# A hybrid encoder block on one core: x transposed through ScalarE's queue, the second FFN product two chunks behind, and transposes in whole groups

## The chip, the core and the metric

The kernel runs on one core of one Trainium2 chip. The time is device microseconds of that core for one execution of the whole block. A core has five engines with a queue each: TensorE (PE in the profile, with PEld for its weight loads), VectorE (DVE), ScalarE (ACT), GpSimd (POOL) and SyncE (SP, which here only issues transfers). Each works through its own queue in order and waits on semaphores of the others.

## The reference

One layer on 256 tokens of width 1024, in float32:

```python
h = rmsnorm(x, ffn1_pre_g);  x = x + 0.5 * rmsnorm(swiglu(h, ffn1_w_in, ffn1_w_down), ffn1_post_g)
h = rmsnorm(x, mix_pre_g);   # one input projection: HGRN2 recurrence and forgetting attention
y = sigmoid(gate_A) * (A @ w_branch_a) + sigmoid(gate_B) * (B @ w_branch_b)
x = x + rmsnorm(y @ w_out, mix_post_g)
x = x + rmsnorm(mem_cross_attention(rmsnorm(x, mem_pre_g), rmsnorm(mem, mem_kv_g), ...), mem_post_g)
h = rmsnorm(x, ffn2_pre_g);  x = x + 0.5 * rmsnorm(swiglu(h, ffn2_w_in, ffn2_w_down), ffn2_post_g)

def swiglu(h, w_in, w_down):
    gate, up = jnp.split(h @ w_in, 2, axis=-1)      # 1024 -> 2 x 2816
    return (jax.nn.silu(gate) * up) @ w_down        # 2816 -> 1024
```

The change touches the head of the kernel (the first norm and the start of the first FFN), both FFNs, and one small step of the mixing stage (the lower bounds of the recurrence's forget gate, a softmax over two rows of logits).

## The kernel before

**Numbers.** Every large product is made of three matmuls: both operands are split into `hi` (rounded to the matmul's format) and `lo` (the rest), and hi x hi, hi x lo and lo x hi are added up in PSUM.

**Weights.** All weights lie in 260 units of 128 x 1024 floats (512 KB). `unit` (L109) issues one transfer on SyncE (L117) into a `raw` tile, casts it to `hi` on ScalarE (L118) and subtracts for `lo` on VectorE (L119). There are 4 `raw` buffers and 8 each of `hi` and `lo`; so a transfer waits until VectorE is done with the unit four before it.

**The norm.** The first product doesn't wait for the norm's statistics. Its input is x^T times the gain (`gain_split`, L245: `hi` on ScalarE, `lo` on VectorE), and the factor per token (`rstd`) is applied when the product is evacuated. `rstd_x` takes the sum of squares of x on ScalarE (L222) and a Newton iteration of small steps on VectorE (L206 to L218).

**The head** (L181 to L216 and L390 to L412): five float32 matmuls of `ones` on TensorE for warming and one Exp on ScalarE; the columns `cols_s` (all gains, the logits of the lower bounds, gate biases) on ScalarE's queue; `fbias` and the masks on GpSimd's. SyncE issues in turn a quarter of x^T and a weight unit, and behind these x itself (`xs`, 1 MB). The lower bounds of the forget gate (`le`, `lbv`, `olb`) follow, with an Exp on ScalarE.

**An FFN** (`ffn`, L288). The 2816 channels go in 11 chunks of 256. A chunk's first product has 24 matmuls of 512 columns per token half h (L153, `proj_tok`); `act_evac` (L298) makes `sg` (Silu on ScalarE) and `at` (times the other half, on VectorE); `act_T` (L305) transposes `at` in two 128 x 128 pieces on TensorE and splits the result into the stationary operand `act` of the second product. `down` (L336) is a chunk's second product, 12 matmuls per half into four PSUM banks `acc`. In the first FFN, `act_first` (L320) does both halves of chunks 0 and 1 together, as units arrive, and chunk 0's evacuation is called right after it. From chunk 1 on the second product of chunk c-1 follows the first product of chunk c; the last four chunks' second products are kept for the end, one token half after the other, so that the closing norm of one half lies beside the other half's matmuls.

**The order.** The tile framework's planner sets each engine's order ahead of the run: of the instructions whose inputs its own estimate of durations has ready, it issues the one with the highest priority, as a rule the earliest in the program. `after(i)` (L80) gives a block high priority and puts its TensorE instructions behind matmul number i of the program; the constants L_ACT = 15, L_F1, L_IA and so on count such matmuls. `late` and `flush` (L294) hold a chunk's transposes back until a later product is being written, with a due place 16 and 17 matmuls into it. PSUM has 4 `acc` banks, 2 `mm` banks and 2 `tr` banks.

Of the kernel before, what the change touches and what calls it, by code (L numbers as in the profile page):

```python
# [9 lines left out]
F32 = mybir.dt.float32  # L10
# [6 lines left out]
P = 128  # L17
# [26 lines left out]
WARM = 5  # L44
# [18 lines left out]
def block_kernel(ctx: ExitStack, tc: tile.TileContext, wts, x_in, xT_in, mem_in, memT_in, cols, rows, fbias, masks, out):  # L63
# [39 lines left out]
    def trp():  # L103
        return pp.tile([P, 512], F32, tag="tr", name=nm("tr"), bufs=2)


    cache = {}

    def unit(name, i, parts=1):  # L109
        u = _AT[name] + i  # L110
        if u not in cache:
            raw = wp.tile([P, D], F32, tag="raw", name=nm("raw"), bufs=4)
            hi = wp.tile([P, D], F32R, tag="hi", name=nm("hi"), bufs=8)
            lo = wp.tile([P, D], F32R, tag="lo", name=nm("lo"), bufs=8)
            for a in range(0, D, D // parts):
                cut = slice(a, a + D // parts)
                nc.sync.dma_start(raw[:, cut], wts[u][:, cut])  # L117
                S.copy(hi[:, cut], raw[:, cut])  # L118
                V.tensor_tensor(out=lo[:, cut], in0=raw[:, cut], in1=hi[:, cut].bitcast(F32), op=ALU.subtract)  # L119
            cache[u] = (hi, lo)  # L120
        return cache[u]
# [65 lines left out]
    S.activation(warm, ones[:, 0:1], AF.Exp)  # L187
    wps = trp()
    for _ in range(WARM):
        MM(wps[:, :P], ones, ones, start=True, stop=True)  # L190
    cols_s = cp.tile([P, 80], F32, name="cols_s")
    S.dma_start(cols_s, cols)
    xs = cp.tile([P, 2, D], F32, name="xs")
    fb_s = cp.tile([8, 1], F32, name="fb_s")
    G.dma_start(fb_s, fbias)
    masks_s = cp.tile([P, len(LEVELS), 64], I32, name="masks_s")
    G.dma_start(masks_s, masks)
# [47 lines left out]
    def gain_split(X, kb, src, g, a=0, b=T):  # L245
        gs = cols_s[:, g + kb : g + kb + 1]
        S.activation(X.hi(kb, a, b), src, AF.Copy, scale=gs)  # L247
        V.scalar_tensor_tensor(out=X.lo(kb, a, b), in0=src, scalar=gs, in1=X.hi(kb, a, b).bitcast(F32), op0=ALU.mult, op1=ALU.subtract)  # L248
# [39 lines left out]
    def ffn(w_in, w_dn, X, r2, n_tok, i_row, first_half, second_half=None):  # L288


        acts = {}
        late = []

        def flush(n):  # L294
            while late:
                late.pop(0)(n)

        def act_evac(ps, c, h):  # L298
            sg = sp.tile([P, FC], F32, tag="c1", name=nm("sg"), bufs=4)
            S.activation(sg, ps[:, :FC], AF.Silu, scale=r2[h])  # L300
            a = sp.tile([P, FC], F32, tag="c1", name=nm("at"), bufs=4)
            V.scalar_tensor_tensor(out=a, in0=ps[:, FC:], scalar=r2[h], in1=sg, op0=ALU.mult, op1=ALU.mult)  # L302
            late.append(lambda m: act_T(a, h, acts[c], m))

        def act_T(a, h, act, m):  # L305
            tr = trp()
            for j in range(2):
                with after(m + 1 + j):
                    PE.transpose(tr[:, j * P : (j + 1) * P], a[:, j * P : (j + 1) * P], ident)  # L309
            with tc.high_priority():  # L310
                split(act[:, 0, :, h * P : (h + 1) * P], act[:, 1, :, h * P : (h + 1) * P], tr[:, :FC].rearrange("p (j t) -> p j t", j=2))
# [8 lines left out]
        def act_first(c, bank):  # L320

            n = len(log)
            u = chunk(w_in, c)
            outs = [bank(), bank()]
            for kb in range(KB):
                wh, wl = blk(u, kb)
                for h in range(2):
                    a, b = h * P, h * P + P
                    MM(outs[h], X.hi(kb, a, b), wh, start=(kb == 0), stop=False)
                    MM(outs[h], X.hi(kb, a, b), wl, start=False, stop=False)  # L330
                    MM(outs[h], X.lo(kb, a, b), wh, start=False, stop=(kb == KB - 1))
            flush(n + L_ACT)
            for h in range(2):
                act_evac(outs[h], c, h)
# [14 lines left out]
        for h in range(2):  # L349
            m = len(log)  # L350
            for c in range(n_tok):
                act_tok(c, h)
            if h == 0 and n_tok:
                second_half(m)
        accs = None
        done = 0
        for c in range(n_tok, NFF):
            acts[c] = m4([P, 2, 2, T], F32R, "act")
            if c < 2:
                act_first(c, (acc, mm)[c])  # L360
            else:
                for h in range(2):
                    act_tok(c, h)
            if c == 6:
                grow = load_row(i_row)
            if accs is None and c:
                accs = [[acc(), acc()], [acc(), acc()]]
            while done < min(c, NFF - STAG):
                n = len(log)
                for h in range(2):  # L370
                    down(done, h)
                done += 1
                flush(n + L_ACT)
# [14 lines left out]

    X1 = Pair()
    for j in range(4):  # L390
        xT = sp.tile([P, 2, T], F32, tag="z2", name=nm("xT"), bufs=3)
        nc.sync.dma_start(xT, xT_in[:, 2 * j : 2 * j + 2, :])
        unit("f1_in", j, 2 if j == 0 else 1)
        for i in range(2):
            gain_split(X1, 2 * j + i, xT[:, i], G_F1)
    for h in range(2):
        nc.sync.dma_start(xs[:, h], x_in[:, h])
    r1 = [rstd_x(x_halves(h)) for h in range(2)]
# [12 lines left out]
    V.tensor_tensor(out=lbv, in0=le[:, 0:8], in1=lsum, op=ALU.mult)  # L411
    V.tensor_scalar(out=olb, in0=lbv, scalar1=-1.0, scalar2=1.0, op0=ALU.mult, op1=ALU.add)  # L412
# [9 lines left out]

    ffn("f1_in", "f1_dn", X1, r1, 0, 0, lambda m: half(X2, r2, 0, G_MIX, m + L_F1))


    iv = [m4([P, 2, 512], n="iv") for _ in range(2)]
    for h in range(2):
        m = len(log)
        for c in range(2):
            ps = mm()  # L430
            proj_tok(ps, X2, chunk("i_a", c), h)
            S.activation(iv[c][:, h, :], ps, AF.Copy, scale=r2[h])
        if h == 0:
            half(X2, r2, 1, G_MIX, m + L_IA)
    row2 = row_of(r2)

# [465 lines left out]
def _layout(inputs):  # L902
# [41 lines left out]
    def col(v):  # L944
# [14 lines left out]
        "wts": wts, "x": nat(a["x"]), "xT": tra(a["x"]), "mem": nat(a["mem"]), "memT": tra(a["mem"]),  # L959
# [19 lines left out]
```

## Time and profile before

| | |
|---|---|
| median of 3 runs | 815.61 us (815.0 to 817.06) |
| the profiled execution | 817.39 us |
| its span, first to last instruction | 815.6 us |
| TensorE busy | 796.6 us, 98% |
| VectorE, ScalarE busy | 522.5 us (64%), 418.5 us (51%) |
| moved by DMA | 146.91 MB, mean 180 GB/s |

Times in the views count from the first instruction. TensorE's busy time is a union of modelled spans; matmuls overlap, so the distance between their starts tells the pace. Lines name the kernel's source (L77 is every matmul, L117 to L119 every weight unit, L309 the transposes of an FFN's chunk, L256 the transposes of x behind a norm); a tile's name tells which operation is meant.

### The profile page before, as it was taken

The page shows a single profiled execution, that of the slowest core. Times are in us where ns is not written, and L with a number is a line of the kernel's source. Part 1 is how long each engine was busy: PE and PEld are TensorE (multiplying, and loading weights), DVE is VectorE, ACT ScalarE, POOL GpSimd, SP SyncE. Part 2 cuts the span into 40 slices and gives each one's busy share as a digit, 9 for nine tenths or more (in the row PEclk, how much of TensorE's full clock was granted, in tenths as well). Part 3 has the DMA queues.
Part 4 walks back from the last instruction along what each step waited for, and adds up shares of the span by engine and source line. Part 5 has one row for each costly group of instructions (what it writes and reads, how often), then busy time and mean ns, then how long its engine had stood idle before and what let it go on. Part 6 is the DMA issues. An engine that isn't in the chain of part 4 may idle for free.

```text
span 815.6 us, 13560 instructions
## 1 busy us (share of the span) xinstructions
PE 796.6 (98%) x5404; PEld 697.3 (85%) x5404; DVE 522.5 (64%) x858; ACT 418.5 (51%) x659; POOL 9.5 (1%) x22
## 2 busy tenths in 40 slices
PE   7999999999999999999999999999999999999996
PEld 5788888887799889998999998999887788888884
DVE  6764555447776897578585466975748755545544
ACT  7644544436565345347675345744636644544531
POOL 0000000000000000100000000000000000000000
PEclk9999999999999999999999999999999999999999
DMA  8675566454464554652466447355426564565421
GB/s 322 244 249 177 173 207 214 161 201 155 151 203 173 174 182 140 201 179 104 155 209 230 149 163 258 134 179 205 153 79 207 190 217 161 185 215 204 168 79 52
DMA packets 41087, 146.91 MB, mean 180 GB/s; under 512 B 4744, under 2 KB 4752, under 8 KB 41024
## 3 DMA queue, kind: packets, MB, share of 16 engines
q1 hardware_dynamic: 40320, 144.20, 51.5%
q0 software_dynamic: 560, 1.81, 0.8%
q8 instruction: 42, 0.69, 0.3%
q14 instruction: 21, 0.17, 0.1%
q10 hardware_dynamic: 144, 0.04, 0.0%
HBM read 144.97 MB, written 1.06 MB: 179 GB/s over the span
## 4 chain that ended last, share of the span: by engine, by line
PE 87%; DVE 5%; DMA 4%; ACT 2%; issue 2%; SPq 0%; DVEq 0%; ACTq 0%
PE mm L77 64%; PE acc L77 20%; DMA raw<-in_wts_dram 3%; DVE lo L119 2%; PE tr L309 1%; PE tr L77 1%; DMA xs<-in_x_dram 1%; ACT junk L222 1%; DVE xs L283 1%; PE tr L256 1%; DVE t L211 1%; DMA cols_s<-in_cols_dram 0%; DVE y L213 0%; ACT hi L118 0%; DVE post L279 0%
## 5 line engine op out<-in xcount | busy, mean ns | idle before, releaser
L119 DVE TENSOR_TENSOR lo<-raw,hi 128x1024 fp32r<-128x1024 f32 (+1 forms) x262 | 317.0, 1221 | 128.1 <-ACT hi L118 124.3
L118 ACT CAST hi<-raw 128x1024 fp32r<-128x1024 f32 (+1 forms) x262 | 269.1, 1046 | 156.8 <-PE mm L77 80.1
L77 PE MATMUL mm<-hi,hT 128*128 128x512 f32 x464 | 183.7, 397 | 2.2 <-ACT hT L247 1.1
L77 PE MATMUL mm<-hT,hi 128*128 128x256 f32 x648 | 183.7, 284 | 0.1
L77 PE MATMUL mm<-hT,lo 128*128 128x256 f32 x648 | 183.7, 284 | 0.0
L77 PE MATMUL mm<-lT,hi 128*128 128x256 f32 x648 | 183.7, 283 | 0.0
L77 PE MATMUL mm<-hi,lT 128*128 128x512 f32 x464 | 183.5, 396 | 0.0
L77 PE MATMUL mm<-lo,hT 128*128 128x512 f32 x464 | 181.5, 391 | 0.5 <-DVE lo L119 0.5
L77 PEld LDWEIGHTS mm<-lT,hi 128*128 128x128 f32 x648 | 124.3, 192 | 0.3 <-issue 0.2
L77 PEld LDWEIGHTS mm<-hT,hi 128*128 128x128 f32 x648 | 124.3, 192 | 0.1
L77 PEld LDWEIGHTS mm<-hT,lo 128*128 128x128 f32 x648 | 124.3, 192 | 0.1
L77 PE MATMUL acc<-hi,act 128*128 128x512 f32 x352 | 114.4, 397 | 0.0
L77 PEld LDWEIGHTS mm<-hi,hT 128*128 128x128 f32 x464 | 87.0, 188 | 22.3 <-ACT hT L247 2.4
L77 PEld LDWEIGHTS mm<-hi,lT 128*128 128x128 f32 x464 | 87.2, 188 | 19.7 <-DVE lT L248 0.3
L77 PEld LDWEIGHTS mm<-lo,hT 128*128 128x128 f32 x464 | 87.2, 188 | 17.6 <-DVE lo L119 1.0
L77 PEld LDWEIGHTS acc<-hi,act 128*128 128x128 f32 x352 | 66.2, 188 | 14.9
L77 PE MATMUL acc<-lo,act 128*128 128x512 f32 x176 | 68.7, 390 | 0.0
L300 ACT ACTIVATE sg<-mm,rstd 128x256 f32<-128x256 f32 x42 | 19.9, 474 | 62.8 <-PE mm L77 62.8
L302 DVE SCALAR_TENSOR_TENSOR at<-mm,rstd,sg 128x256 f32<-128x256 f32 x42 | 20.1, 480 | 49.7 <-ACT sg L300 49.6
L77 PEld LDWEIGHTS acc<-lo,act 128*128 128x128 f32 x176 | 33.1, 188 | 6.3
L77 PE MATMUL acc<-hi,hT 128*128 128x512 f32 x80 | 32.0, 405 | 2.8 <-ACT hi L118 2.7
L77 PE MATMUL acc<-lo,hT 128*128 128x512 f32 x80 | 31.8, 398 | 0.3 <-DVE lo L119 0.3
(176 smaller groups left out, 634.4 us busy)
## 6 DMA issues: line engine op xcount, KB each, us to landing
raw<-in_wts_dram SPq DMA_DIRECT2D x260, 512.0 KB, 4.5
grow<-in_rows_dram SPq DMA_DIRECT2D x4, 512.0 KB, 5.7
xT<-in_xT_dram SPq DMA_DIRECT2D x4, 256.0 KB, 5.2
xs<-in_x_dram SPq DMA_DIRECT2D x2, 512.0 KB, 7.4
cbm<-cd POOLq DMA_DIRECT2D x2, 512.0 KB, 7.0
memT<-in_memT_dram SPq DMA_DIRECT2D x2, 512.0 KB, 7.1
ms<-in_mem_dram SPq DMA_DIRECT2D x2, 512.0 KB, 6.3
out_dram<-xs SPq DMA_DIRECT2D x4, 256.0 KB, 2.0
```

What stands on the lines that cost most here:

```text
L77: log.append(PE.matmul(*args, **kw).ins)
L118: S.copy(hi[:, cut], raw[:, cut])
L119: V.tensor_tensor(out=lo[:, cut], in0=raw[:, cut], in1=hi[:, cut].bitcast(F32), op=ALU.subtract)
L211: V.scalar_tensor_tensor(out=t, in0=v, scalar=y, in1=y, op0=ALU.mult, op1=ALU.mult)
L222: S.activation(junk[:, : src.shape[-1]], src, AF.Square, accum_out=dst)
L256: PE.transpose(ps[:, j * P : (j + 1) * P], src(kb), ident)
L283: V.scalar_tensor_tensor(out=xh, in0=t, scalar=r, in1=xh, op0=ALU.mult, op1=ALU.add)
L300: S.activation(sg, ps[:, :FC], AF.Silu, scale=r2[h])
L302: V.scalar_tensor_tensor(out=a, in0=ps[:, FC:], scalar=r2[h], in1=sg, op0=ALU.mult, op1=ALU.mult)
L309: PE.transpose(tr[:, j * P : (j + 1) * P], a[:, j * P : (j + 1) * P], ident)
```

## The change

Head: x^T comes in four tiles of its own in the data pool, on ScalarE's queue, its first quarter in two transfers; each 128-channel block of 256 tokens has one more column that holds the gain, so that `gain_split` takes its scale from there and no longer from `cols_s`. The first block's `hi` is made on VectorE. The warming has seven matmuls, and the early activation is a Silu. x is issued behind the seventh weight transfer (unit 5), and the columns, `fbias` and the masks behind unit 7, all on SyncE. Chunks 0 and 1 of the first FFN go into the four `acc` banks and are evacuated after both; `norm_1` calls the statistics in between. In `act_first` the order of a block's matmuls is now hi, lo of x with `wh`, then `wl`, both halves side by side.

FFNs: the second product of chunk c-2 (before: c-1) follows the first product of chunk c. A chunk's four transposes go into one PSUM bank, behind one due matmul, with one split of 512 columns; `late` holds chunks, and `flush` takes one at a time. `sg` and `at` have 7 buffers (before: 4).

Mixing: the lower bounds are written behind the projection `i_a`, their Exp behind its last evacuation.

```diff
-WARM = 5
+WARM = 7
+X_AT = 6
...
-                nc.sync.dma_start(raw[:, cut], wts[u][:, cut])
+                loads.append(nc.sync.dma_start(raw[:, cut], wts[u][:, cut]).ins)
...
+        if first:
+            V.tensor_scalar(out=X.hi(kb, a, b), in0=src, scalar1=gs, scalar2=None, op0=ALU.mult)
+        else:
+            S.activation(X.hi(kb, a, b), src, AF.Copy, scale=gs)
...
         def flush(n):
-            while late:
-                late.pop(0)(n)
+            if late:
+                c = late.pop(0)
+                tr = trp()
+                trv = tr.rearrange("p (j t) -> p j t", j=2)
+                with after(n):
+                    for h in range(2):
+                        for j in range(2):
+                            PE.transpose(trv[:, j, h * P : (h + 1) * P], ats[c, h][:, j * P : (j + 1) * P], ident)
+                    split(acts[c][:, 0], acts[c][:, 1], trv)
 
         def act_evac(ps, c, h):
...
+            ats[c, h] = a
+            if h == 1:
+                late.append(c)
 
         def act_tok(c, h):
-            n = len(log)
             ps = mm()
             proj_tok(ps, X, chunk(w_in, c), h)
-            flush(n + L_ACT)
             act_evac(ps, c, h)
...
             for c in range(n_tok):
+                n = len(log)
                 act_tok(c, h)
+                flush(n + L_ACT)
...
+        if callable(r2):
+            outs = [act_first(c) for c in range(2)]
+            r2 = r2()
+            for c in range(2):
+                acts[c] = m4([P, 2, 2, T], F32R, "act")
+                for h in range(2):
+                    act_evac(outs[c][h], c, h)
+            n_tok = 2
         for c in range(n_tok, NFF):
             acts[c] = m4([P, 2, 2, T], F32R, "act")
-            if c < 2:
-                act_first(c, (acc, mm)[c])
-            else:
-                for h in range(2):
-                    act_tok(c, h)
+            for h in range(2):
+                n = len(log)
+                act_tok(c, h)
+                if c == 2 or c > NFF - STAG + 1:
+                    flush(n + L_ACT)
...
-            while done < min(c, NFF - STAG):
+            while done < min(c - 1, NFF - STAG):
                 n = len(log)
                 for h in range(2):
                     down(done, h)
+                flush(n + L_ACT)
                 done += 1
-                flush(n + L_ACT)
...
     X1 = Pair()
+    xT = [m4([P, 2, T + 1], n="xT") for _ in range(KB // 2)]
+    for kb in range(2):
+        S.dma_start(xT[0][:, kb], xT_in[:, kb])
+    for j in range(1, 4):
+        S.dma_start(xT[j], xT_in[:, 2 * j : 2 * j + 2])
+    S.activation(warm, ones[:, 0:1], AF.Silu)
+    wps = trp()
+    for _ in range(WARM):
+        MM(wps[:, :P], ones, ones, start=True, stop=True)
     for j in range(4):
-        xT = sp.tile([P, 2, T], F32, tag="z2", name=nm("xT"), bufs=3)
-        nc.sync.dma_start(xT, xT_in[:, 2 * j : 2 * j + 2, :])
         unit("f1_in", j, 2 if j == 0 else 1)
         for i in range(2):
-            gain_split(X1, 2 * j + i, xT[:, i], G_F1)
+            gain_split(X1, 2 * j + i, xT[j][:, i, :T], xT[j][:, i, T:], first=2 * j + i == 0)
+
+    def norm_1():
+        with tc.issue_after(loads[X_AT]):
+            for h in range(2):
+                nc.sync.dma_start(xs[:, h], x_in[:, h])
+        with tc.issue_after(loads[-1]):
+            nc.sync.dma_start(cols_s, cols)
+            nc.sync.dma_start(fb_s, fbias)
+            nc.sync.dma_start(masks_s, masks)
+        return [rstd_x(x_halves(h)) for h in range(2)]
...
-    S.activation(le, le, AF.Exp)
+    with tc.issue_after(iv_last):
+        S.activation(le, le, AF.Exp)
```

More of the change, by code (lines that the diff above doesn't have):

```diff
@@ L107, in block_kernel @@
     cache = {}
+    loads = []
     def unit(name, i, parts=1):
@@ L186, in block_kernel @@
     warm = s1(name="warm")
[L187 to L190, printed above, removed]
+    xs = cp.tile([P, 2, D], F32, name="xs")
     cols_s = cp.tile([P, 80], F32, name="cols_s")
-    S.dma_start(cols_s, cols)
-    xs = cp.tile([P, 2, D], F32, name="xs")
     fb_s = cp.tile([8, 1], F32, name="fb_s")
-    G.dma_start(fb_s, fbias)
     masks_s = cp.tile([P, len(LEVELS), 64], I32, name="masks_s")
-    G.dma_start(masks_s, masks)
     junk = cp.tile([P, 512], F32, name="junk")
@@ L243, in row_of, with gain_split @@
         return row
[L245 to L247 removed]
+    def gain_split(X, kb, src, g, a=0, b=T, first=False):
+        gs = cols_s[:, g + kb : g + kb + 1] if isinstance(g, int) else g
+        if first:
+            V.tensor_scalar(out=X.hi(kb, a, b), in0=src, scalar1=gs, scalar2=None, op0=ALU.mult)
+        else:
+            S.activation(X.hi(kb, a, b), src, AF.Copy, scale=gs)
         V.scalar_tensor_tensor(out=X.lo(kb, a, b), in0=src, scalar=gs, in1=X.hi(kb, a, b).bitcast(F32), op0=ALU.mult, op1=ALU.subtract)
@@ L305, in act_T @@
[L305 to L311, printed above, removed]
+            ats[c, h] = a
+            if h == 1:
+                late.append(c)
         def act_tok(c, h):
-            n = len(log)
@@ L412, in block_kernel @@
     V.tensor_scalar(out=olb, in0=lbv, scalar1=-1.0, scalar2=1.0, op0=ALU.mult, op1=ALU.add)
-    X2 = Pair()
-    r2 = [None, None]
-    def half(X, r, h, g, m):
-        with after(m):
-            to_T(X, x_blocks(h), h, g)
-        r[h] = rstd_x(x_halves(h))
[L423 to L435, printed above, removed]
     wh, wl = unit("f_b", 0)
```

47 lines of the change are left out of this document (29 added, 18 removed).

## The prediction

> **What bounds the kernel now.** I read the page first, then what TensorE waited for, then the timeline of the first 40 us, and last the chain of waits in the places that the diff touches.
>
> ```profile
> PE 796.6 (98%) x5404; PEld 697.3 (85%) x5404; DVE 522.5 (64%) x858; ACT 418.5 (51%) x659; POOL 9.5 (1%) x22
> ```
>
> TensorE is busy for 98% of the span, so a change gains only where TensorE stands idle. The view of TensorE's waits lists nearly all of that:
>
> ```profile
> PE acc L77 <- ACT hi L118: 2.7, 1, 2.7
> PE tr L309 <- DVE at L302: 1.9, 2, 1.0
> PE tr L256 <- DVE xs L283: 1.2, 2, 1.0
> PE mm L77 <- ACT hT L247: 1.1, 2, 1.0
> PE mm L77 <- ACT hi L118: 1.1, 1, 1.1
> ```
>
> The columns are total us, times, longest us. The first, fifth and sixth rows lie in the head, and one of the two L309 waits too. Here is the head's timeline (start, duration, engine, line; in brackets the idle time before and what ended it):
>
> ```profile
> 0.75 0.41 ACTq L192 DMA_DIRECT2D cols_s<-in_cols_dram  x1
> 4.77 0.91 ACT L247 ACTIVATE hT<-xT,cols_s 128x256 fp32r<-128x256 f32 x2 [2.08 <-DMA cols_s<-in_cols_dram]
> 6.23 1.22 PE L77 MATMUL acc<-hi,hT 128*128 128x512 f32 x2 [2.67 <-ACT hi L118]
> 8.11 0.63 PE L77 MATMUL acc<-lo,hT 128*128 128x512 f32 x1
> 8.53 0.63 PE L77 MATMUL acc<-hi,lT 128*128 128x512 f32 x1
> 9.09 1.05 ACT L118 CAST hi<-raw 128x1024 fp32r<-128x1024 f32 x1 [1.00 <-DMA raw<-in_wts_dram]
> 10.05 0.90 ACT L247 ACTIVATE hT<-xT,cols_s 128x256 fp32r<-128x256 f32 x2
> 10.17 1.23 DVE L119 TENSOR_TENSOR lo<-raw,hi 128x1024 fp32r<-128x1024 f32 x1 [1.28 <-ACT hi L118]
> 10.59 0.61 PE L77 MATMUL acc<-hi,hT 128*128 128x512 f32 x2
> 11.45 0.50 PE L77 MATMUL acc<-lo,hT 128*128 128x512 f32 x1 [0.25 <-DVE lo L119]
> ```
>
> Work begins at 6.23, on weight unit 0; unit 1 is used from 10.59. Early matmuls start 0.42 us apart. Chunk 0 ends at 19.34 (last start 19.11 plus one pitch):
>
> ```profile
> 14.28 0.64 ACT L222 ACTIVATE junk<-xs 128x512 f32<-128x512 f32 x1 [0.22 <-DMA xs<-in_x_dram]
> 17.81 1.28 ACT L300 ACT_TABLE_LOAD   x1 [0.54 <-DVE rstd L218]
> 19.11 0.39 PE L77 MATMUL acc<-hi,lT 128*128 128x512 f32 x1
> 19.42 0.15 DVE L218 TENSOR_SCALAR rstd<-y 128x1 f32<-128x1 f32 x1
> 19.48 1.03 ACT L118 CAST hi<-raw 128x1024 fp32r<-128x1024 f32 x1
> 20.57 0.73 PE L77 MATMUL mm<-hi,hT 128*128 128x512 f32 x2 [1.07 <-ACT hi L118]
> 21.83 0.50 PE L77 MATMUL mm<-lo,hT 128*128 128x512 f32 x1 [0.53 <-DVE lo L119]
> ```
>
> ScalarE has waited 0.54 for the first `rstd` when it loads the Silu table; it does the first Silu and only then casts unit 4, for which TensorE waits. From the first square at 14.28 to the second `rstd` at 19.57 the statistics of x take 5.3. Line 309's transposes wait once more:
>
> ```profile
> 37.99 0.33 PE L309 MATMUL tr<-ident,at 128*128 128x128 f32 x1 [0.96 <-DVE at L302]
> ```
>
> **The change, part by part.**
>
> *Chunk 0's start.* ScalarE issues five x^T transfers at 0.41 us (row at 0.75), then the table load of 1.28: free at about 4.1 and a small step more, ahead of its first cast (before, its first input came at 4.77). SyncE loses the x^T issues, so unit 0 is issued first. The scale rides in x^T, so the wait for `cols_s` is gone; the lower-bound steps leave both queues, and VectorE takes one `hT` (half of 0.90) from ScalarE. Bytes moved per us, from 0 (40 slices of 1 us):
>
> ```profile
> GB/s 0 25 138 213 335 347 360 395 422 410 410 412 406 426 393 414 410 422 393 229 4 0 66 303 258 303 139 287 340 385 377 180 270 250 143 360 205 250 295 299
> ```
>
> Before, ahead of unit 1's end lie units 0 and 1, half of x^T, masks and columns: 1.84 MB, reached at 8.06 by summing the row; the cast followed at 9.09, 1.0 later. Now x^T (1.05 MB) shares the engines with units 0 to 3 (2.10 MB). If bytes are shared in step, unit 1 and its x^T are complete at 1.57 MB, 7.4 on the row, so 8.4 with that lag, and units 2 and 3 at 10.3 and 12.3. Then ScalarE needs a pair of `hT` (0.90) and a cast (1.05): unit 1 starts near 10.3, against 10.59. Its `lo` follows 1.23 later; the new order puts four matmuls ahead of the first `wl`, 0.9 us, so 0.3 is waited where 0.6 was. Chunk 0 ends about 0.5 earlier. Bounds: 1.5 earlier if unit 1 is cast at 9.4 and unit 0 done by then; 1.0 later if x^T holds unit 1 back by 1.5. I take -0.5.
>
> By the Trainium skill, "DMA: Bandwidth & Descriptors", section "Issuing engines are not separate DMA queues", transfers from different engines run on the same DMA engines and a second one saves only issue time; the sum with no gain from the queue would be 0.5 worse, 812.8. Before has no such pair of streams in its traffic, so the traces leave this open.
>
> *From chunk 0's end to the second product's first end.* Two windows, TensorE's matmuls of line 77 and its transposes of line 309:
>
> ```profile
> 19.34:39.98 20.64, 17.88 (x73) 13.45 (x73) 1.00 0.67 233
> 19.34:39.98 20.64, 1.74 (x8) 1.12 (x8) 1.00 0.67 233
> ```
>
> One of the 73 began earlier, so 72 matmuls and 8 transposes. Their prices come from the chain of waits:
>
> ```profile
> 40.15 9.32 PE mm L77 x41
> ...
> 49.47 0.11 PE tr L309
> 49.58 0.24 PE mm L77
> 49.82 0.11 PE tr L309
> ```
> ```profile
> 379.23 0.87 PE tr L256 x8
> ```
>
> A matmul is 9.32 / 41 = 0.227; two lone transposes and the matmul between take 0.46, so 0.116 each. 72 x 0.227 + 8 x 0.116 = 17.3 of 20.64: 3.3 us are lost. After, chunks 0 and 1 run through with no evacuation between them, the Silu table is loaded in the head, and 48 more matmuls stand ahead of the second product. x comes after two more units: 5.25 MB, near 17.4 by the row's 0.41 MB per us; with the 5.3 of statistics both `rstd` are there near 22.7, and chunk 0's transposes are due near 32. Unit 4, issued when unit 0's buffer is free (about 7.5), lands near 13.5 and is cast ten matmuls or more ahead of its use. What would be late next is chunk 2's weights, which land by about 26 for a use at 29. I take -3.3; bounds -3.3 and -1.6, if ScalarE is again held behind x for a cast (1.07 + 0.53 remain).
>
> *Longer warming* adds four passes at 0.25 us on an idle TensorE (its ten took 2.5), ending near 4.6, ahead of the first real matmul: nothing on the path. *Masks and columns later:* after unit 7, first needed far behind; nothing, for three issues of 0.41 go into SyncE's wait for buffers (without it, 1.2 us in front of unit 8's issue, which has 3 to spare). *The Exp of the bounds after the input projection:* its table load comes earlier on ScalarE and the later one of the forget logit goes; nothing, as weights are cast ahead.
>
> *Groups.* In a group of eight a transpose takes 0.109, alone 0.116: 0.007 x 4 x 15 chunks that go as one group = 0.4. ScalarE and VectorE split a chunk in one go, off the path; that the second product follows two chunks behind costs nothing, since it only orders the same matmuls and leaves the split a chunk's time. Bounds 0 and -0.8. I take -0.4.
>
> *The second FFN's stall.* TensorE waits for the first chunk's `at`, late behind the table load:
>
> ```profile
> 630.70 0.44 PE L309 MATMUL tr<-ident,at 128*128 128x128 f32 x2 [0.95 <-DVE at L302]
> ```
>
> This transpose now comes after the other half. But the same VectorE queue yields the second token half right then, so I take -0.6 of it; bounds 0 and -0.95.
>
> *Flushed at once.* In `act_tok`'s loops a chunk enters `late` and is flushed in the same step: chunks 9 and 10 of each FFN, and 0, 1, 2 of the second. The due place (15 matmuls into the chunk's second half) has passed already, so the planner's own estimate of when `at` is ready decides, and on the chip TensorE waits for the difference with everything queued behind. Two groups in the trace stand by such an estimate: x's transposes after the first FFN, due after 19 and 23 matmuls and placed after some 26 and 39.
>
> ```profile
> 192.26 0.63 PE L256 MATMUL tr<-ident,xs 128*128 128x128 f32 x4 [0.21 <-issue]
> ```
> ```profile
> 198.20:209.40 11.20, 9.34 (x40) 7.07 (x39) 1.00 0.60 213
> ```
> ```profile
> 209.48 0.66 PE L256 MATMUL tr<-ident,xs 128*128 128x128 f32 x4 [0.98 <-DVE xs L283]
> ```
>
> They waited 0.21 and 0.98. The way to `at` is two instructions, much shorter than a norm, so nearer the first: 7 x 0.21 = +1.5. Bounds 0 and 6.9.
>
> **The sum:** -0.5 - 3.3 - 0.4 - 0.6 + 1.5 = -3.3 us. The profiled execution took 817.39 us (span 815.6), 1.8 over the median of 815.61; it would become 814.1, and the median 812.3. About 0.3%, 2.4 us, can be told from no change.
>
> **The rivals.**
>
> *All of it and the clock early.* Waits of 0, unit 1 at its early bound: -1.5 - 3.3 - 0.4 - 0.9 = -6.1, 809.5. For it: matmuls 0.42 apart still at 8.5 show that the old warming did not outlast the idle 2.67; fourteen passes end closer to the first matmul. Against: unit 1's bytes, not the clock, set when it starts. By the Trainium skill, "TensorE: Matmul & The Clock Gate", Part 1, a busy window of about 3.4 us gives full clock; the trace agrees as to the two paces (a pair of matmuls takes 1.22 at 6.23 and 0.61 at 10.59), and by that rule 3.5 us of warming might do alone, which would make this rival likelier.
>
> *x^T holds the weights back.* The 2:1 sharing fails and unit 1 is 1.5 late: +1.0 - 3.3 - 0.4 + 1.5 = -1.2, 814.4, no measurable change. For it: the engines move 0.41 MB per us from 7 on and are full; against: masks leave the head.
>
> *The planner is too eager (slower).* The place is the seven flushed chunks. In the ninth chunk:
>
> ```profile
> 163.68 0.47 ACT L300 ACTIVATE sg<-mm,rstd 128x256 f32<-128x256 f32 x1 [0.17 <-PE mm L77]
> ...
> 164.76 0.47 DVE L302 SCALAR_TENSOR_TENSOR at<-mm,rstd,sg 128x256 f32<-128x256 f32 x1
> ```
>
> `at` ends at 165.23, 1.95 after the next chunk's matmuls began (sg starts 0.4 into them). Put straight behind the chunk, each group costs 1.95: 13.7 - 4.8 = +8.9, 824.5. It ends slower from (4.8 + 2.4) / 7 = 1.04 per group. Against: no wait in the trace is that long outside the head.
>
> **How the numbers follow.** The forecast has 0.5, the full gain 0.17, the held weights 0.18, the eager planner 0.13, 0.02 is left. The forecast's own range is 810.5 to 814, a fifth of it within 0.3%: faster 0.5 x 0.85 + 0.17 = 0.6, same 0.08 + 0.18, slower 0.14. The range 809.3 to 816.8 holds the first three and the eager planner's mild part.
>
> **What would show it.** TensorE's first `acc` matmul near 5.4 and unit 1 near 10.3; no wait between 13 and 40 us; no table load near 17; in the waits, L309's successor with seven entries of about 0.2; groups of four in the second products. It is wrong if a cast in the head waits for x, if unit 1 comes after 11, or if those entries pass 1 us.

## The result, and the profile after

| | before | after |
|---|---|---|
| median on one chip | 816.21 us (815.0 to 817.06, 5 runs) | 812.74 us (811.94 to 812.88, 5 runs) |
| ratio, with its 95% interval | | 0.995 (0.9933 to 0.9968) |
| the profiled execution (its span) | 817.39 (815.6) | 812.33 (810.5) |

The changed kernel is faster by 3.5 us between the medians and by 5.1 us between the two profiled executions. The forecast was 3.3 less, 812.3.

In the changed kernel line 79 is every matmul, 121 a weight unit's cast and 122 its `lo`, 246 and 247 make `hT` and `lT` from x^T, 302 is a group of transposes, 307 and 309 make `sg` and `at`, 255 transposes x. The page of the changed kernel, the row of busy times:

```profile
PE 795.7 (98%) x5408; PEld 698.1 (86%) x5408; DVE 523.6 (65%) x837; ACT 415.0 (51%) x635; POOL 8.8 (1%) x20
```

TensorE's busy time is 0.9 less than before (796.6); the other 4.2 of the 5.1 us are idle time. What TensorE waited for in the changed kernel (total us, times, longest):

```profile
PE acc L79 <- ACT hi L121: 1.4, 1, 1.4
PE tr L255 <- DVE xs L282: 1.1, 2, 0.9
PE tr L79 <- DVE ones L185: 1.1, 1, 1.1
PE mm L79 <- issue: 0.8, 1, 0.8
PE acc L79 <- DVE lT L247: 0.5, 1, 0.5
PE acc L79 <- ACT hT L246: 0.4, 1, 0.4
PE tr L302 <- DVE at L309: 0.4, 1, 0.4
PE mm L79 <- DVE lT L247: 0.4, 1, 0.4
```

The 2.7 for the first cast became 1.4; the 1.9 for `at` became 0.4; the waits for unit 4 are gone. Four rows are new: 0.4 for `hT` and 0.5 for `lT` in the head, 0.8 for "issue" (time in which TensorE waited for nothing that the profile shows), 0.4 for `lT` at the second FFN. The head's timeline after:

```profile
3.40 1.28 ACT L403 ACT_TABLE_LOAD   x1 [3.40 <-issue]
5.84 0.71 PE L79 MATMUL acc<-hi,hT 128*128 128x512 f32 x2 [1.44 <-ACT hi L121]
8.07 1.05 ACT L121 CAST hi<-raw 128x1024 fp32r<-128x1024 f32 x1 [0.90 <-DMA raw<-in_wts_dram]
9.02 0.90 ACT L246 ACTIVATE hT<-xT 128x256 fp32r<-128x256 f32 x2
9.58 0.73 PE L79 MATMUL acc<-hi,hT 128*128 128x512 f32 x2 [0.45 <-ACT hT L246]
10.83 0.50 PE L79 MATMUL acc<-hi,lT 128*128 128x512 f32 x1 [0.52 <-DVE lT L247]
14.33 1.99 ACT L121 CAST hi<-raw 128x1024 fp32r<-128x1024 f32 x2
18.69 0.62 PE L79 MATMUL acc<-hi,hT 128*128 128x512 f32 x2
```

Unit 1's weights are cast from 8.07 (before: 9.09). Behind unit 3, ScalarE casts units 4 and 5 from 14.33, long before chunk 0 ends; chunk 1 begins at 18.69 without a gap. TensorE from there to 39.5 us in the view of windows (start and end, length, PE busy with its instructions, clock, DMA share, GB/s):

```profile
18.69:39.50 20.81, 20.81 (x98) 1.00 0.85 291
```

It is busy for all of the window. For a table by stretch, marks that both traces have are x's transposes behind the first FFN and ahead of the second; after, then before for the second of them (before's first one, 192.26, stands in the prediction):

```profile
188.17 0.52 PE L255 MATMUL tr<-ident,xs 128*128 128x128 f32 x3 [0.21 <-issue]
```
```profile
608.55 0.52 PE L255 MATMUL tr<-ident,xs 128*128 128x128 f32 x3 [0.25 <-DVE xs L282]
```
```profile
613.42 0.63 PE L256 MATMUL tr<-ident,xs 128*128 128x128 f32 x4 [0.26 <-DVE xs L283]
```

| stretch, ending at (before, after) | gained in it | the prediction's terms for it |
|---|---|---|
| chunk 0 (19.34, 18.69) | 0.65 | 0.5 |
| the rest of the first FFN (192.26, 188.17) | 3.44 | 3.3 + 0.2 for groups - 0.4 for chunks 9 and 10 = 3.1 |
| projection, mixing, attention (613.42, 608.55) | 0.78 | 0 |
| second FFN (815.62, 810.54) | 0.21 | 0.6 + 0.2 for groups - 1.1 for five chunks = -0.3 |

(In the last column the prediction's terms are split by chunks: 9 of the 15 whole groups and 2 of the 7 chunks "flushed at once" lie in the first FFN.)

### The profile page after: what moved, and what is told of

Its sections match the earlier page's. It is cut to its first block, busy times and chain, and to the rows that moved or that the text cites. A ratio compares the mean times of both kernels' runs of the same rounds, so it can differ in the third digit from the quotient of the medians.

```text
span 810.5 us, 13507 instructions
## 1 busy us (share of the span) xinstructions
PE 795.7 (98%) x5408; PEld 698.1 (86%) x5408; DVE 523.6 (65%) x837; ACT 415.0 (51%) x635; POOL 8.8 (1%) x20
## 4 chain that ended last, share of the span: by engine, by line
PE 89%; DVE 4%; DMA 2%; issue 2%; ACT 1%; SPq 0%; DVEq 0%; ACTq 0%
PE mm L79 63%; PE acc L79 23%; DMA raw<-in_wts_dram 2%; DVE lo L122 2%; PE tr L302 1%; PE tr L79 1%; ACT junk L218 1%; DVE xs L282 1%; PE tr L255 1%; DVE t L207 1%; DVE y L209 0%; ACT hi L121 0%; DVE post L278 0%; PE tr L711 0%; PE tr L881 0%
## 5 line engine op out<-in xcount | busy, mean ns | idle before, releaser
L79 PE MATMUL mm<-lo,hT 128*128 128x512 f32 x448 | 175.9, 393 | 0.0
L79 PE MATMUL mm<-hi,hT 128*128 128x512 f32 x448 | 175.6, 392 | 0.0
L79 PE MATMUL mm<-hi,lT 128*128 128x512 f32 x448 | 175.0, 391 | 0.4 <-DVE lT L247 0.4
L79 PE MATMUL acc<-hi,act 128*128 128x512 f32 x352 | 111.6, 390 | 0.0
L79 PEld LDWEIGHTS mm<-hi,lT 128*128 128x128 f32 x448 | 84.2, 188 | 18.4 <-DVE lT L247 1.1
L79 PEld LDWEIGHTS mm<-hi,hT 128*128 128x128 f32 x448 | 84.1, 188 | 17.9 <-ACT hT L246 0.5
L79 PEld LDWEIGHTS mm<-lo,hT 128*128 128x128 f32 x448 | 84.2, 188 | 16.7
L79 PE MATMUL acc<-hi,hT 128*128 128x512 f32 x96 | 35.3, 395 | 2.0 <-ACT hi L121 1.4
L79 PE MATMUL acc<-hi,lT 128*128 128x512 f32 x96 | 35.2, 393 | 0.5 <-DVE lT L247 0.5
```

The lines of the kernel that those rows point to most:

```text
L79: log.append(PE.matmul(*args, **kw).ins)
```

## The experiments

Each stands beside runs of the kernel before on the same chip, whose medians there were 815.32 to 816.29. Ratios are to those, with 95% intervals.

**The head alone.** The changed kernel's head with the FFNs of before: transposes in pairs, the second product one chunk behind.

```diff
-                    split(acts[c][:, 0], acts[c][:, 1], trv)
+            while late:
+                late.pop(0)(n)
...
-            while done < min(c - 1, NFF - STAG):
+            while done < min(c, NFF - STAG):
```

> The changed kernel with the FFNs' old pattern put back (single transposes, second product one chunk behind); the head stays changed. Theory: the gain is the head's (chunk 0 ends at 18.7 instead of 19.3, and the 3.3 us of waits from there to the first second product are gone), so about 4 us under the kernel before, 812.2, and 0.5 or less from the changed kernel's 812.7. Rival (the order of the second products and the groups carry it): 815 or more. In the trace the theory wants no wait of TensorE between 13 and 36 us.

Measured: 813.62 us, 0.997 (0.996 to 0.9979), so 2.7 of the 3.5 us are the head's. That is 1.4 above the 812.2 that the theory wanted, so by the medians the FFNs' order is worth about 0.8 on this head, where the theory gave it 0.5 at most. Chunk 0 ends at 18.99. It has a wait that the changed kernel lacks, of the transposes for the buffer that the split of the chunk before frees:

```profile
36.89 0.44 PE L308 MATMUL tr<-ident,at 128*128 128x128 f32 x2 [0.48 <-DVE act L136]
```

**The FFNs alone.** Groups, two chunks behind, in the kernel with the old head.

```diff
-            if accs is None and c:
+            if accs is None and c > 1:
...
-            while done < min(c, NFF - STAG):
+            while done < min(c - 1, NFF - STAG):
```

> The kernel before with the FFNs' new pattern alone (groups of four, two chunks behind); head as before. Theory: 0.4 from the groups and 0.3 to 0.6 from the second FFN's first wait, so 815.3 to 815.8 against 816.2, within what can be told from no change. Rival: 813, most of the gain.

Measured: 817.87 us, 1.0019 (1.0009 to 1.0028): slower than before, which neither theory nor rival had. A new wait stands at chunk 1's end (TensorE's timeline, then ScalarE's):

```profile
32.66 0.39 PE L77 MATMUL mm<-hi,lT 128*128 128x512 f32 x1
34.22 1.20 PE L77 MATMUL acc<-hi,act 128*128 128x512 f32 x4 [1.17 <-ACT hi L118]
...
36.28 0.40 PE L77 MATMUL mm<-hi,hT 128*128 128x512 f32 x1
```
```profile
33.12 1.04 ACT L118 CAST hi<-raw 128x1024 fp32r<-128x1024 f32 x1 [0.28 <-DMA raw<-in_wts_dram]
34.07 0.47 ACT L309 ACTIVATE sg<-mm,rstd 128x256 f32<-128x256 f32 x1
```

Chunk 1 holds both `mm` banks until it is evacuated (its two `sg` start at 34.07 and 35.40), so chunk 2's product cannot begin, and a second product whose weights are cast at that moment stands in its place.

**The FFNs alone, chunk 1 in accumulators.** The run before with one word changed, to test that reading.

```diff
-                act_first(c, (acc, mm)[c])
+                act_first(c, acc)
```

> The FFN's part of the change alone on the head of the kernel before, and chunk 1 of the first FFN in accumulator banks too, like chunk 0 (in the run of the FFN's part alone it took both mm banks). Theory (that part alone lost because chunk 1 held the mm banks, so that chunk 2's first product could not begin and a second product with weights just arrived came first): the wait of 1.17 near 34 us is gone and the time falls from 817.9 to 816 to 816.6. Rival (the loss comes from the second products two chunks behind, with the old head's late weights): a wait of over 1 us for 'ACT hi' stays between 30 and 40 us, and the time is 817.5 or more.

Measured: 815.74 us, 1.0004 (0.999 to 1.0017). The wait at 34 is gone; against their own neighbours the two runs stand at +1.6 and +0.4 us, so it was worth about its 1.2, as far as medians with such intervals tell. What the FFNs' new order needs is the four banks; on the old head it then comes out even, since the waits behind chunk 0 are still there.

**Shorter warming.**

```diff
-WARM = 7
+WARM = 5
```

> The changed kernel with five warming matmuls instead of seven. By my prediction's step (warming is worth nothing, the arrival of unit 1 sets the pace) chunk 0 ends within 0.3 of 18.7 and the time stays at 812.7. Rival (the clock): the first matmuls are 0.42 apart until about 9.4, unit 0's twelve then end at 10.4 instead of 9.0, and chunk 0 ends 0.7 to 1.5 later, time 813.4 to 814.2.

Measured: 813.74 us, 0.997 (0.9958 to 0.9982). TensorE's head:

```profile
5.34 1.22 PE L79 MATMUL acc<-hi,hT 128*128 128x512 f32 x2 [1.77 <-ACT hi L121]
...
8.91 0.92 PE L79 MATMUL acc<-hi,lT 128*128 128x512 f32 x2
9.67 0.63 PE L79 MATMUL acc<-lo,hT 128*128 128x512 f32 x2
10.14 0.63 PE L79 MATMUL acc<-hi,hT 128*128 128x512 f32 x2
```

A pair takes 1.22 and starts every 0.85 until 8.9, where the changed kernel's takes 0.7 and 0.54. Still unit 1 is begun at 10.14 and chunk 0 ends at 18.60, against 18.69: the slow matmuls of unit 0 fill time in which unit 1 is not ready. So chunk 0 ends where the theory has it, but the time is the rival's. The gain on its neighbours is 0.9 smaller than the changed kernel's; its trace has two larger waits far from the head, which other runs have too, 1.0 for `at` and 1.0 for `hT` at the input projection (below). They would cover the 0.9; that the other executions have them too is not shown.

**x^T on SyncE's queue.** As before the change, but with the scale column.

```diff
-    for kb in range(2):
-        S.dma_start(xT[0][:, kb], xT_in[:, kb])
-    for j in range(1, 4):
-        S.dma_start(xT[j], xT_in[:, 2 * j : 2 * j + 2])
...
+            nc.sync.dma_start(xT[j], xT_in[:, 2 * j : 2 * j + 2])
```

> The changed kernel with x^T issued on SyncE in turn with the weight units, as before, all else changed. Theory: the bytes ahead of unit 1 are what matters, masks and columns are still later, so the first matmul is up to 0.5 later and chunk 0 ends within 0.5 of 18.7; 812.7 to 813.2. Rival (the second queue is the gain of the head's start): chunk 0 ends at 19.3 or later, 813.4 or more.

Measured: 813.91 us, 0.9978 (0.9965 to 0.9991). Unit 1 begins at 10.25 instead of 9.58, and chunk 0 ends at 18.91, 0.22 later than in the changed kernel. ScalarE's queue is worth about that at its place. The time is again the rival's, though chunk 0 is the theory's: the trace has a wait for `at` of 1.1 and one for "issue" of 1.4, together some 1.2 more than the changed kernel's, which would cover the rest.

**Chunk 0 evacuated between the two chunks**, as before the change, x issued two units earlier.

```diff
-            outs = [act_first(c) for c in range(2)]
+            outs = [act_first(0), None]
             r2 = r2()
             for c in range(2):
+                if c:
+                    outs[1] = act_first(1)
```

> Changed kernel, but chunk 0 of the first FFN is evacuated before chunk 1's first product is called, as in the kernel before; for this x is issued two weight units earlier. Theory (the time of the head's second part, 3.3 us, was lost because ScalarE handled x and chunk 0's evacuation ahead of the casts of chunk 1's units): part of the loss returns; TensorE waits between chunk 0's end and 40 us for at least 1.5 us in all, with a row on 'ACT hi' or 'DVE lo' near 19 to 22, and the time is 814.2 to 816. Rival (what mattered was that both chunks have accumulators of their own and that the Silu table is loaded already; the place of the evacuation in the order is nothing): no wait over 0.3 us before 40 us, and the time is within 0.6 us of the run with x earlier alone, some 812.8.

Measured: 813.24 us, 0.9978 (0.9967 to 0.9989). The theory fell: behind chunk 0 TensorE waits 0.2 once, and never again before 180 us. The rival's time is missed by 0.6; the trace has a wait of 1.4 for `at` in the second FFN, where the run with x early has 0.8. ScalarE:

```profile
16.94 0.19 ACT L218 ACTIVATION_READ_ACCUMULATOR junk<-xs 128x1 f32 x1
17.04 1.99 ACT L121 CAST hi<-raw 128x1024 fp32r<-128x1024 f32 x2
18.93 0.46 ACT L307 ACTIVATE sg<-acc,rstd 128x256 f32<-128x256 f32 x1
```

All four squares of x still lie ahead of unit 4's cast, but the first Silu now stands behind it.

**x early.** The changed kernel with x at that earlier place alone.

```diff
-X_AT = 6
+X_AT = 4
```

> Changed kernel, but x is issued behind the fifth weight transfer (unit 3) and no longer behind the seventh (unit 5), as early as in the kernel before; everything else stays. Theory (the prediction's step that x's place in the traffic is worth nothing, as chunk 1's units have time to spare): TensorE's row of waits stays free between 11 and 40 us, and the time is 812.7, give or take 0.6. Rival (the change's gain comes from x later: 1 MB ahead of units 4 to 7 is 2.5 us of the full traffic at 0.41 MB per us): TensorE waits 1 to 2.5 us for 'ACT hi' of a unit of chunk 1 between 18 and 26 us, and the time is 814 to 815.

Measured: 812.03 us, 0.9959 (0.9944 to 0.9974). No wait between 11.5 and 180 us. For the changed kernel x's place in the traffic is worth nothing.

**The Silu table in the head, in the kernel before.**

```diff
-    S.activation(warm, ones[:, 0:1], AF.Exp)
+    S.activation(warm, ones[:, 0:1], AF.Silu)
...
+    with tc.issue_after(iv_last):
+        S.activation(le, le, AF.Exp)
```

> Kernel before, with two of the change's parts alone: the early activation is a Silu and the lower bounds (with their Exp) come behind the input projection, so that the Silu table is loaded in the head and not in the middle of chunk 0. Theory (the wait of 1.07 + 0.53 after chunk 0 came from ScalarE's order, where the first Silu stands ahead of the cast of unit 4: that Silu needs chunk 0's last matmuls near 19.1 whether or not the table is loaded): the table load near 17.8 is gone, the cast of unit 4 still starts near 19.5, TensorE waits as long as before behind chunk 0, and the time is 815.3, give or take 0.7. Rival (the table load of 1.28 held the cast back): the cast starts by 18.3, the wait behind chunk 0 is under 0.4 and the time is 813.7 to 814.2.

Measured: 815.32 us, 1.0 (0.999 to 1.001).

```profile
18.72 0.47 ACT L300 ACTIVATE sg<-acc,rstd 128x256 f32<-128x256 f32 x1 [1.52 <-PE acc L77]
19.09 2.93 ACT L118 CAST hi<-raw 128x1024 fp32r<-128x1024 f32 x3
```
```profile
20.18 0.73 PE L77 MATMUL mm<-hi,hT 128*128 128x512 f32 x2 [0.82 <-ACT hi L118]
21.44 0.50 PE L77 MATMUL mm<-lo,hT 128*128 128x512 f32 x1 [0.53 <-DVE lo L119]
```

The table load is gone and ScalarE stands idle in its place: the first Silu reads an accumulator, so it waits for the last matmul of its token half (18.29 in this trace), and unit 4's cast behind it in the queue waits too. Without the table load that cast starts 0.39 earlier than before (19.09 for 19.48) and TensorE's wait is 0.25 shorter; the medians don't show it.

**Two units ahead of x, in the kernel before.** One line: units 4 and 5 are loaded and cast ahead of the statistics.

```diff
+    for j in range(4, 6):
+        unit("f1_in", j)
     for h in range(2):
         nc.sync.dma_start(xs[:, h], x_in[:, h])
```

> Kernel before, with one line: weight units 4 and 5 (the first half of chunk 1) are loaded and cast ahead of x and its statistics; the Silu table is still loaded in the middle, and nothing else of the change is there. Theory (the wait behind chunk 0 is ScalarE's order, the first Silu ahead of unit 4's cast; x's place matters only as it sets that order): the waits of 1.07 and 0.53 at 20.57 and 21.83 are gone, chunk 1 goes on at full pace, and the time is 813.6 to 814.4. Rival (x's statistics then come 2.5 us later, so the first Silu, chunk 0's transposes and the mm banks do too, and the wait moves to chunk 1's end): a new wait of 1 us or more for ACT or DVE between 24 and 40 us, and the time is 815 or more.

Measured: 813.1 us, 0.9968 (0.9957 to 0.9979), 2.3 us below its neighbours. ScalarE and TensorE:

```profile
15.98 1.05 ACT L118 CAST hi<-raw 128x1024 fp32r<-128x1024 f32 x1 [0.78 <-DMA raw<-in_wts_dram]
18.06 0.64 ACT L222 ACTIVATE junk<-xs 128x512 f32<-128x512 f32 x1 [1.03 <-DMA xs<-in_x_dram]
...
21.60 1.28 ACT L300 ACT_TABLE_LOAD   x1 [0.54 <-DVE rstd L218]
22.89 0.47 ACT L300 ACTIVATE sg<-acc,rstd 128x256 f32<-128x256 f32 x1
```
```profile
19.46 0.39 PE L77 MATMUL mm<-hi,hT 128*128 128x512 f32 x1
```

With the table load and the wait for `rstd` still in the middle, TensorE begins chunk 1 one pitch behind chunk 0's last matmul (19.23), and its view of waits is empty from 11.5 to 180 us. This one line removes those waits, and with them two thirds of what the whole change gains. It moves the two transfers as well as the casts, but the transfer of unit 4 was not what came late: in the kernel before it was issued at 8.32 and took (last number, us)

```profile
raw<-in_wts_dram SPq DMA_DIRECT2D x1, 512.0 KB, 8.5
```

so it had landed near 16.8, 2.7 ahead of its cast at 19.48. ScalarE was done with the squares of x by 17.3.

**The due place of the groups.** The changed kernel, but the chunks that are flushed in the step that makes them get their transposes 15 matmuls into the next product.

```diff
-        def act_tok(c, h):
+        def act_tok(c, h, fl):
+            n = len(log)
             ps = mm()
             proj_tok(ps, X, chunk(w_in, c), h)
+            if fl:
+                flush(n + L_ACT)
             act_evac(ps, c, h)
...
         for c in range(NFF - STAG, NFF):
+            if c == NFF - 1:
+                flush(m + L_ACT)
             down(c, 0)
-        flush(m + L_ACT)
```

> Changed kernel, but the chunks that are flushed in the step in which they are made (9 and 10 of both FFNs, 0, 1 and 2 of the second) get their transposes in the next product, 15 matmuls into it, as in the kernel before; still in groups of four. Theory (the prediction's step that such a group waits because the planner's own estimate alone places it): the wait of TensorE on line 302's or 305's transposes for 'DVE at' (0.4 in the changed kernel's second FFN, 1.1 and 1.2 in three of the four runs so far) is gone, no such row stays, and the time is 0.4 to 1.0 below the changed kernel's 812.7. Rival (the wait comes from VectorE's and ScalarE's load in the second FFN, wherever the transposes are due): a row of 0.4 or more stays near 628 to 650 us and the time is the same.

Measured: 811.04 us, 0.995 (0.9934 to 0.9966), 1.0 below the run with x early beside it. From 600 to 700 us, around the second FFN's start, its longest wait is

```profile
PE mm L79 <- DVE lT L247: 0.6, 1, 0.6
```

and none is for `at`. Its interval overlaps the changed kernel's, so what speaks for it is the missing row. The next run has the same due places and stands 0.9 below the changed kernel itself on the same chip.

**x^T split ahead of the cast**, on top of that.

```diff
-        unit("f1_in", j, 2 if j == 0 else 1)
+        if j == 0:
+            unit("f1_in", j, 2)
         for i in range(2):
             gain_split(X1, 2 * j + i, xT[j][:, i, :T], xT[j][:, i, T:], first=2 * j + i == 0)
+        if j:
+            unit("f1_in", j)
```

> Due places as in the earlier run with the later due place, and besides, in the head, each quarter of x^T but the first is scaled and split ahead of its weight unit's cast, in the time in which ScalarE waits for the weights. Theory (unit 1's start is held by ScalarE's and VectorE's work behind the weights: 0.61 and 0.69 of TensorE's idle time near 8.7 and 9.9 in the changed kernel): the wait for lT near 10 is gone, chunk 0 ends 0.4 to 0.9 earlier, and the time is 810.2 to 810.7 beside 811.0. Rival (the weights' arrival bounds chunk 0, so the time saved at unit 1 is waited at unit 2 or 3): chunk 0 ends within 0.2 of 18.5 and the time is 811.0.

Measured: 811.11 us, 0.9943 (0.9931 to 0.9955): nothing.

```profile
8.16 0.91 ACT L246 ACTIVATE hT<-xT 128x256 fp32r<-128x256 f32 x2 [1.09 <-DMA xT<-in_xT_dram]
...
8.98 1.03 ACT L121 CAST hi<-raw 128x1024 fp32r<-128x1024 f32 x1
```

The second quarter of x^T arrives at about the time of unit 1, so the cast moves from 8.07 to 8.98; the wait for `lT` near 10 is gone, unit 1 begins at 10.06, chunk 0 ends at 18.71. The time is the rival's. What took the gain here is x^T's arrival at unit 1; that the weights bound chunk 0 behind it is not shown.

**The changed kernel once more.**

> The changed kernel itself once more, beside the others on the same chip, to tell which of its waits come back: theory (the late weight at the input projection, the wait of line 302 in the second FFN and the wait for instructions in the mixing stage differ from run to run by up to 1 us each): the median within 0.6 of 812.5, line 302's row between 0.4 and 1.4. Rival (they belong to the kernel): the same rows as in its first profile, within 0.1 each.

Measured: 811.99 us, 0.9955 (0.9943 to 0.9968). Chunk 0 ends at 18.69 again; the wait for `at` is 0.5, that for "issue" 0.8. Over all runs of the changed order in the second FFN (after, shorter warming, x^T on SyncE, evacuation between, x early, once more) the wait for `at` was 0.4, 1.0, 1.1, 1.4, 0.8 and 0.5. This run alone does not decide: these two rows came back within 0.1, as the rival has it, while another wait for "issue", near 289 us, went from 0.3 to 0.9. But in all six traces TensorE, ScalarE, VectorE and SyncE do the same instructions in the same order throughout the second FFN, so there the order of the kernel does not make the difference.

## Why the prediction was right, and where it was not

**Chunk 0's start: right, by a slightly other way.** It gained 0.65 for 0.5. The prediction had unit 1's cast at 8.4 and it came at 8.07. It asked for a whole pair of `hT` before the first matmul (10.3); the first of the two is enough (9.58). It expected 0.3 of waiting for unit 1's `lo`; what came late is `lT` (0.52), since VectorE makes the unit's `lo` first. By the Trainium skill, "DMA: Bandwidth & Descriptors", section "Issuing engines are not separate DMA queues", a second queue saves issue time only; with x^T on SyncE's queue 0.43 of the 0.65 stay, so the trace agrees in the main: the queue was worth 0.22.

**The warming: right.** Shorter warming leaves chunk 0's end where it was (18.60). The longer one does reach full pace earlier: at 5.5 to 6.2 us in six of the eight traces with seven matmuls, at 8.8 and 9.9 in the other two, and at 9.3 to 11.5 in all six with five. By the Trainium skill, "TensorE: Matmul & The Clock Gate", Part 1, the window of some 3.4 us runs freely, so the moment differs from run to run; the head alone and the changed kernel, with the same head and full pace from 9.9 and 6.2, agree with it. The profile's granted clock reads 1.00 in all these stretches; the pace is read from the distance between starts (0.43 us, then 0.23). The rival "all of it and the clock early" is thus refuted in its clock: it came early and was worth nothing.

**The 3.3 behind chunk 0: right in size, wrong in two of its three reasons.** The stretch gained 3.44. Of that the head alone gained 2.66 and the FFNs' order the rest. The prediction gave the missing evacuation, the table load in the head and the 48 matmuls ahead of the second product together. The evacuation can stay in between (0.2 waited), and the table load moved alone gains nothing in the medians. The waits of 1.07 and 0.53 were ScalarE's order: a Silu that needs chunk 0's last matmuls stood ahead of a cast that needed nothing. Its bound of -1.6 did foresee that a cast held on ScalarE would keep them, but it blamed x for that; in the run with chunk 0 evacuated in between, all of x's squares stand ahead of the cast and nothing is lost. Its own rows came near it: the cast at 19.48 follows a Silu that reads the accumulator and so could not start before some 18.9, with or without the 1.28 of table (the last matmul of its half starts at 18.43; in the run with the table early the Silu began 0.43 behind that matmul). The 0.96 for `at` at 37.99, which the prediction put to the 48 matmuls, goes without them in the run with the two units first; on the changed head the FFNs' old order still loses 0.64 at that place (36.89).

**x later: right.** The second half of x was issued only at 15.46, behind unit 7, so the second `rstd` is there at 25.4 and not at the 22.7 of the prediction. ScalarE does wait for x, but behind the casts of units 4 to 7, and it costs nothing. In the kernel before, the same move pays because it puts the casts ahead.

**Groups: between 0.1 and 0.3 in the first FFN, where the prediction had 0.2.** From chunk 1's end to x's transposes, with equal work:

```profile
29.87:189.25 159.38, 158.50 (x675) 124.89 (x673) 1.00 0.58 193
```
```profile
29.57:188.17 158.60, 156.61 (x675) 125.38 (x673) 1.00 0.59 194
```
```profile
29.37:187.83 158.46, 156.14 (x675) 125.53 (x673) 1.00 0.58 195
```

These are the head alone, the changed kernel and the later due place (line 79's matmuls; each has 44 transposes besides). The first holds the wait at 36.89, 0.64 more than a pitch of 0.23 behind the matmul before it (36.02); 159.38 - 0.64 - 158.60 = 0.1, and 0.3 against the third.

**Flushed at once: the term that was mis-sized.** The prediction had seven entries of 0.21, 1.5 in all. One of the seven waits, in the second FFN:

```profile
642.29 0.44 PE L302 MATMUL tr<-ident,at 128*128 128x128 f32 x2 [0.42 <-DVE at L309]
```

and the others not at all: the planner splits each of the seven groups in two and puts 15 matmuls between the halves (19 in this one). So the term was 0.4 here and up to 1.4 in other runs. What makes `at` late is the same in all six traces. Its Silu stands on ScalarE right behind a weight unit's cast, and that cast waits for the unit's transfer; here in the changed kernel, then in the run with chunk 0 evacuated in between:

```profile
639.53 1.05 ACT L121 CAST hi<-raw 128x1024 fp32r<-128x1024 f32 x1 [0.90 <-DMA raw<-in_wts_dram]
640.48 0.47 ACT L307 ACTIVATE sg<-mm,rstd 128x256 f32<-128x256 f32 x1
```
```profile
640.58 1.05 ACT L121 CAST hi<-raw 128x1024 fp32r<-128x1024 f32 x1 [1.87 <-DMA raw<-in_wts_dram]
643.34 0.44 PE L302 MATMUL tr<-ident,at 128*128 128x128 f32 x2 [1.40 <-DVE at L309]
```

Over the six traces, by size, the cast waited 0.90, 1.02, 1.25, 1.42, 1.50 and 1.87, and the transposes for `at` 0.4, 0.5, 0.8, 1.0, 1.1 and 1.4, in the same order. The mechanism of the rival "the planner is too eager" is real at this one place: putting the due place back removed the row, and the two runs that have it stand 0.9 and 1.0 below their partners on the same chips. It never came near the seven times 1.04 that it needed.

**The second FFN's stall: right.** The wait of 0.95 went, and as the prediction feared, the same engines yield the second half late; the price is a wait for `lT`, so 0.56 for 0.6:

```profile
627.30 0.50 PE L79 MATMUL mm<-hi,lT 128*128 128x512 f32 x1 [0.39 <-DVE lT L247]
```

**The 0.78 in between was not foreseen and belongs mostly to the run.** Before's profile has a wait at the input projection, the changed kernel's one in the mixing stage:

```profile
201.42 0.50 PE L77 MATMUL mm<-hi,hT 128*128 128x512 f32 x1 [0.97 <-ACT hT L247]
```
```profile
302.79 0.39 PE L79 MATMUL mm<-hT,lo 128*128 128x256 f32 x1 [0.82 <-issue]
```

The rest is a second wait for "issue" (0.52 before, 0.28 after) and 0.1 at x's transposes (0.98, 0.89). The wait at the input projection comes back with other kernels of both kinds (1.0 to 1.3 in 4 of 14 profiles: before, shorter warming, FFNs alone with accumulators, two units first). The traces differ by 5.1 and the medians by 3.5 because the profiled execution of before lay 1.2 above its median and the changed kernel's 0.4 below. The three stretches that the change touches gained 4.3 in these two traces, 1.0 more than the sum of 3.3, which is the 1.1 that the flushed chunks were priced too high. In the six traces named above their wait is 0.87 in the mean, twice that of this one, so the trace that is compared here was a lucky one. That the median hit within 0.4 is partly the luck of such waits: a price too high for the flushed chunks stood against waits elsewhere that no term of the sum has.

## What to carry to other kernels

When TensorE waits for a cast, look at what stands ahead of that cast on its own engine and what that waits for: here a Silu waiting for TensorE itself held the weights of the next product, and two units cast earlier were worth 2.3 of the 3.5 us that the whole change gains. A reordering that keeps more results pending needs the banks for them; without these it was slower than before (817.87 us against 816.29). And one profiled execution carries waits of a microsecond that the next one lacks, so compare a term at its own place in two traces and the total in medians.

## What the runs showed of the hardware that was not expected

- SyncE's issue of unit 2 waited for x^T, on another queue (its waits, 0 to 30 us):

```profile
SPq L120 <- DMA xT<-in_xT_dram: 3.2, 1, 3.2
```

  While it waited, eight transfers had been issued on both queues together, each with a landing semaphore of its own; the ninth takes the semaphore of the first x^T again (both are number 100 in the trace) and went out at 5.33, as that x^T landed at 5.31. The kernel before does the same: its ninth on these two queues takes the semaphore of `cols_s` and waits for it (0.7). So what holds it is the program's reuse of semaphores; no limit of a queue is shown. It cost nothing here: the unit was cast by 11.87, for a use at 13.2.
- The wait for "issue" near 302 us, where TensorE has just run 128 matmuls of 16 columns in 1.3 us (from 300.32), was between 0.4 and 1.4 in the rows of the changed head's kernels. A transfer of 16 KB of instructions begins near 300.6 in the changed kernel's trace. Its queue makes 42 of them, one for some 258 of TensorE's 10,816 matmuls and weight loads, so it is probably TensorE's; that TensorE waits for it is only argued.
